# A hybrid decoder block in single precision: the second half of the tokens begins with the values of two heads, and three smaller edits

## The chip, the cores and the metric

The kernel runs on one core of one Trainium2 chip. A core has four engines that compute: TensorE (PE: matrix products and transposes into the accumulator memory PSUM), VectorE (DVE), ScalarE (ACT) and GpSimd (POOL). Transfers between the on-chip memory and DRAM are issued from the instruction queue of an engine; SyncE (SP) does nothing else. The metric is device time in microseconds (us), the median of several runs.

## The reference

One layer works on x of 1024 tokens x 2048 columns in float32:

```python
h = rmsnorm(x, ln_g)
proj = h @ w_in                    # columns for three groups and their gates
# group A: gMLP spatial gating in chunks of 128 tokens, 4 groups of 128
# group B: gated DeltaNet, 8 heads of 128: causal conv + SiLU on q, k, v;
#          per chunk T = (I + A)^-1, then a scan over the chunks carries a state
# group C: cross-attention into 256 memory tokens, 4 heads of 128
mixed = concat([out_a, out_b, out_c]) * SiLU(gates)
y = rmsnorm(x + mixed @ w_out, final_g)
```

The change lies in group B. For a head, `q`, `k` and `v` are each a projection of 128 columns, followed by a causal convolution of four taps. Inside a chunk the delta rule needs the inverse of a unit triangular matrix. The scan `S_t` runs over the tokens in order, so the second half of the tokens needs the state of the first.

## The kernel before, in words

**Precision.** Every product of the projections is done as three products (`triple`, line 445): an operand is split into a high part (`hi`, a rounded copy, made by ACT) and a low part (`lo`, the rest, made by DVE), and hi x hi, hi x lo and lo x hi are added in PSUM.

**Order of the work.** The program is first written down as a list of operations with their dependencies. `Plan.price` (line 182) gives each a cost and a latency, and `Plan.issue` (line 222) replays the list: each engine takes, of the operations that its prices call ready, the one of lowest rank (`with rank(n)`; matmuls of the projections have 9, the rest 5 unless said otherwise), and at equal rank the earlier in the program. The order found so is fixed, and every engine works through its own list in that order, waiting where a result isn't there yet. All instructions are issued from one line, so the profile shows line 277 (L277) for nearly everything; groups are told apart by tile names.

**Two halves of the tokens, heads 0 to 3.** The first 512 tokens of h lie split in `ahi` and `alo` (16 pieces of 128 rows each). In the first half heads 0 and 1 are projected (`front(0, 0)`, line 1138), then heads 2 and 3 (`front(1, 0)`), then the values of all four (`values`, line 1181). Each column of 128 is `project` (line 849): 16 pieces x 3 matmuls of 128 x 512 into one of two PSUM banks (`main_bank`), with weights loaded into the `wraw` ring of four and split into `whi` and `wlo` of five each (`w_parts`, line 830). `conv` (line 888) copies the bank into one of three `xr` buffers, so that the bank is free, and convolves from there: q into one of four `qT` slots, k into one of four `kT` slots, one for each head, values into one of four `tn` buffers.

**The chain of a pair of heads.** `qk` (line 924) makes the decays and the products k k and k q; it uses both `inv` buffers. `blocks_out` (line 967) writes 32 x 32 blocks to DRAM (`gdr`), `inverse` (line 980) loads them into an `inv` buffer, inverts 32 blocks at once with 31 steps of two DVE operations each (`y<-inv,inv` and `inv<-inv,y`), and writes the results to DRAM (`tdr`, `udr`). `levels` (line 1008) puts them together, and `scan_step` (line 1079) runs the four chunks. `back` (line 1191) is levels, the scan and `heads_out`. A pair's `qT` and `kT` slots are free for the other half when its scan is over. The inverse has rank 3, below the splits of operands, which have rank 2.

**The step to the second half** (lines 1216 to 1239). `refill` loads one piece of the second half's h from DRAM and splits it into `ahi` and `alo` as soon as the last column of the first half has used that piece. The first two columns of the second half are q and k of head 0, projected together, and each piece's refill and two matmuls of the decays stand ahead of their products (`before`, line 1225). Then follow `decays(1, a)`, the rest of `front(0, 1)` (q and k of head 1), the inverse "10", `back` of heads 2 and 3 of the first half, the values of heads 0 and 1, and heads 2 and 3 of the second half. Between columns `next_job` puts in one of the jobs of `todo`; here these are `left_sums`, which load, add and store pieces for a later stage.

**Low parts.** A column of weights is used in both halves. In `w_parts` the low part of a column of heads 2 and 3, and of the values of all heads, is stored in DRAM in the first half and loaded in the second; q and k of heads 0 and 1 are split anew.

**Later stages**, which the change touches only by the order and by the inverse's transfers: heads 4 to 7 and the other groups are projected in blocks with a scheme of seven products in place of eight (`seven`), the late inverse works on four pairs at once, and the output projection and the norm end the kernel.

Of the kernel before, what the change touches and what calls it, by code (L numbers as in the profile page):

```python
# [17 lines left out]
P = 128  # L18
# [44 lines left out]
class Plan:  # L63
# [117 lines left out]
    def price(self, o, name, outs, ins):  # L181

        out = outs[0]
        n = math.prod(out.shape[1:])
        both = [*outs, *ins]
        psum = any(i.space == PSUM for i in both)
        pointer = any(i.shape[-1] == 1 and math.prod(i.shape[1:]) == 1 for i in ins[1:])
        o.nbytes = o.lock = 0
        o.lat = 0.0
        if name == "dma_start":  # L190
            o.cost = {"sp": 380.0, "act": 100.0, "pool": 800.0}[o.eng]
            rows = math.prod(out.shape[:-1])
            o.nbytes = max(4 * math.prod(out.shape), 512 * rows)
            src = ins[0]
            pieces = src.shape[-1] < 128 or out.shape[-1] < 128
            if out.space == DRAM:
                o.lat = 3000.0
            elif pieces or out.shape[0] < 32:
                o.lat = 2400.0
            elif list(src.ap)[0][0] == 0:  # L200
                o.lat = 4000.0
        elif o.eng == "pe":
            passes = 1 if ins[0].dtype == F32R else 2 if name == "transpose" else 4
            o.cost = max(13.3 + n / 2.4 * passes, 110.0) if out.shape[0] == P else 30.0
            o.lat = 175.0
        elif o.eng == "act":
            o.cost = (165.0 if psum else 200.0) + 0.82 * n + (105.0 if pointer else 0.0)
            o.cost += 190.0 if "accum_out" in o.kw else 0.0
        elif o.eng == "dve":
            n = max([n] + [math.prod(i.shape[1:]) for i in ins])  # L210
            o.cost = (n + 151) / 0.96 + (60.0 if pointer and name == "scalar_tensor_tensor" else 0.0)
            o.lock = not psum and (name.startswith("tensor_") or name == "scalar_tensor_tensor")
            o.lock = o.lock and name != "tensor_reduce"
        else:
            o.lock = 1
            if name in ("memset", "affine_select"):
                o.cost = 100.0 + 0.83 * n * (1 if name == "memset" else 1.4)
                o.lat = 800.0 if name == "affine_select" else 0.0
            else:
                o.cost = 750.0 + 150.0 * (n - 1) if n < 8 else 200.0 + 2.1 * n  # L220

    def issue(self):
        free = dict.fromkeys(self.SEEN, 0.0)
        soon = {e: [] for e in free}
        now = {e: [] for e in free}
        held = {"dve": 0.0, "pool": 0.0}
        dma = 0.0
        for o in self.ops:
            if o.n == 0 and o.lead is o:
                heapq.heappush(soon[o.eng], (0.0, o.idx))  # L230
        left = len(self.ops)
        while left:
            best = None
            for e in free:
                if now[e]:
                    t = free[e]
                elif soon[e]:
                    t = max(free[e], soon[e][0][0])
                else:
                    continue  # L240
                if best is None or t < best[0]:
                    best = (t, e)
            t, e = best
            while soon[e] and soon[e][0][0] <= t:
                i = heapq.heappop(soon[e])[1]
                heapq.heappush(now[e], (self.ops[i].cls, i))
            head = self.ops[heapq.heappop(now[e])[1]]
            for o in (head, *head.tail):
                t = max(t, free[e])
                o.at = t  # L250
                left -= 1
                if o.lock:
                    t = max(t, held["pool" if e == "dve" else "dve"])
                end = t + o.cost
                if o.lock:
                    held[e] = end
                free[e] = end - min(self.OVERLAP[e], 0.5 * o.cost)
                done = end + o.lat
                if o.nbytes:
                    dma = max(dma, end) + o.nbytes / self.DMA_RATE  # L260
                    done = dma + self.DMA_FIXED + o.lat
                for s in o.succ:
                    if s.eng != e or o.nbytes:
                        when = done + self.SEEN[s.eng] + (self.SLACK if s.eng == "pe" else 0.0)
                    elif e == "pe":
                        when = free[e]
                    else:
                        when = end + 34.0
                    s.ready = max(s.ready, when)
                    s.n -= 1  # L270
                    if s.n == 0:
                        heapq.heappush(soon[s.eng], (s.ready, s.idx))
            if len(head.tail) > 7:
                free[e] += self.SWITCH
        self.ops.sort(key=lambda o: (o.at, o.idx))
        for o in self.ops:
            o.fn(*o.args, **o.kw)  # L277
# [3 lines left out]
def kernel(  # L281
# [543 lines left out]
            Q.dma_start(gcs[hf].rearrange("t h p -> (t h) p"), gr)  # L825


    low_d, todo = {}, []

    def w_parts(c0, kp):  # L830

        src = w_in[kp * KP * P : (kp + 1) * KP * P, c0 : c0 + P].rearrange("(k p) c -> p k c", p=P)
        raw = raw_piece(src)
        if (c0, kp) in low_d:
            hi, lo = whi(), wlo()
            with rank(2):
                S.copy(hi, raw)
            with rank(4):
                Q.dma_start(lo.bitcast(F32), low_d[c0, kp])
        else:  # L840
            hi, lo = split_piece(raw)
            if (c0 - C_Q) % DW < 2 * P and c0 < C_DV:
                return [tok(hi), tok(lo)]
            low_d[c0, kp] = DT([P, HT], f"low{c0}_{kp}")
            with rank(6):
                Q.dma_start(low_d[c0, kp], lo.bitcast(F32))
        return [tok(hi), tok(lo)]
# [40 lines left out]
    def conv(which, h, hf, o, a=None):  # L888
        ct = which * NH + h
        xr = ring["xr"]()  # L890
        w = [cw[:, k * 24 + ct : k * 24 + ct + 1] for k in range(4)]
        if h < NJ:
            if a is None:
                last = (which, h, hf) == (2, NJ - 1, 1)
                a = project([column(which, h)], order=(1, 0, 2, 3) if last else range(KT // KP))[0]
            next_job()
            with rank(1):
                S.copy(xr[:, 0:3], halo[:, ct])
                S.copy(xr[:, 3:], a)
# [12 lines left out]
        t = ring["tn"]()  # L912
        S.activation(t, o, AF.Tanh)
        V.scalar_tensor_tensor(o, t, 1.0, o, op0=ALU.add, op1=ALU.mult)
# [52 lines left out]
    def blocks_out(gt, n):  # L967
# [3 lines left out]
        for b in range(4):  # L971
            sl = slice(b * 32, (b + 1) * 32)
            with rank(1):
                Q.dma_start(gdr[b].rearrange("c j i -> j c i"), gv[sl, :, sl])
        return gdr

    def flat(start, *aps):
# [2 lines left out]
    def inverse(gdrs, n, cls):  # L980
# [3 lines left out]
        for i, gdr in enumerate(gdrs):  # L984
            for b in range(4):
                with rank(1):
                    flat(Q.dma_start, gd[i * 32 + b * 8 : i * 32 + (b + 1) * 8], gdr[b])
        ti = ring["inv"]()[0:nr].rearrange("p (a b) -> p a b", b=32)
        tmp = (y1 if nr == 32 else y2)[0:nr].rearrange("p c m -> p (c m)")
        with rank(4):  # L990
# [10 lines left out]
        tdr, udr = ([DT([32, 32, 32], f"{t}{n}_{i}") for i in range(len(gdrs))] for t in ("tdr", "udr"))  # L1001
        for i in range(len(gdrs)):
            with rank(1):
                flat(Q.dma_start, tdr[i], ti[i * 32 : (i + 1) * 32])
                flat(Q.dma_start, udr[i], gd[i * 32 : (i + 1) * 32])
        return list(zip(tdr, udr))

    def levels(gt, tdr, udr):
# [177 lines left out]
            by_token(rest[i][2], to_tokens((v, bank))[0], hss[i][:, 4])  # L1186

    def inverted(n, *states):
        return [(*s[:-1], i) for s, i in zip(states, inverse([s[-1] for s in states], n, 3))]

    def back(hf, hp, gt, qs, ks, hss, rest, inv, ut=None):
        ut = ut or levels(gt, *inv)
# [34 lines left out]
        decay_mm(a, k)  # L1227

    todo += [lambda j=j: left_sums(j) for j in range(NJ, NH)]
    first = project([column(0, 0), column(1, 0)], before)  # L1230
    decays(1, a)
    (state,) = inverted("10", front(0, 1, first))
    back(*ahead)
    ut = levels(state[2], *state[-1])
    values(*state)
# [545 lines left out]
```

## Time and profile before

| | us |
|---|---|
| three runs | 1644.93, 1648.33, 1648.26 (median 1648.26) |
| the profiled execution | 1647.33 |
| its span, from the first to the last instruction | 1645.6 |
| mean granted TensorE clock | 0.997 |

A row of busy time says how long an engine worked and the share of the span. Matmuls are pipelined: a product of 512 columns is shown with 0.39 us, and the next starts 0.23 us after it. A wait row has the engine that waited, what it waited for, the sum, the number of times and the longest. A window row has, for a stretch of the span, the busy time of PE, PEld (weight loads of TensorE), DVE, ACT and POOL, each with its number of instructions, then the granted clock, the DMA engines' share and GB/s. "SPq" and "ACTq" are the instruction queues of SyncE and ScalarE.

### The profile page before, as it was taken

To read this page: it belongs to the slowest core of one execution; us is meant where nothing else is said; L and a number is where in the kernel's file an instruction comes from. 1 tells how busy PE (TensorE), PEld (TensorE's weight loads), DVE (VectorE), ACT (ScalarE), POOL (GpSimd) and SP (SyncE) were. 2 spreads that over 40 slices of the span, in tenths; PEclk is the share of its full clock that TensorE was granted. 3 is DMA by queue.
4 is the path that set the end of the run, shared out by engine and by line. 5 is a ranking of instruction groups with operands and counts; after the bars stand their busy time and mean duration, and the time that the engine had idled before them with its cause. 6 is when DMAs were issued, how large, how long until landed. Compare 5 with 4: busy or idle time off the path is not lost.

```text
span 1645.6 us, 26195 instructions
## 1 busy us (share of the span) xinstructions
PE 1615.4 (98%) x8570; PEld 1354.1 (82%) x8570; DVE 1323.4 (80%) x2288; ACT 1025.8 (62%) x2235; POOL 117.1 (7%) x139
## 2 busy tenths in 40 slices
PE   8999999899999999999999999999999999999997
PEld 6888887788888888888888787888888888888886
DVE  4866796767879869899999898879678898688875
ACT  6957764576846446877686546766657774344445
POOL 0001110210200000100101101000000000000001
PEclk9999999999999999999999999999999999999999
DMA  8989888586887877579877887889778789678646
GB/s 265 257 233 278 261 275 258 178 247 200 265 287 238 265 236 231 183 266 331 303 229 243 293 277 208 276 281 303 249 240 279 258 281 352 200 269 300 220 143 241
DMA packets 316659, 419.51 MB, mean 255 GB/s; under 512 B 57773, under 2 KB 138342, under 8 KB 316522
## 3 DMA queue, kind: packets, MB, share of 16 engines
q1 hardware_dynamic: 314818, 414.67, 77.7%
q0 software_dynamic: 1088, 2.10, 0.5%
q8 instruction: 67, 1.10, 0.3%
q10 hardware_dynamic: 616, 1.07, 0.2%
q14 instruction: 70, 0.57, 0.1%
HBM read 334.33 MB, written 82.87 MB: 254 GB/s over the span
## 4 chain that ended last, share of the span: by engine, by line
PE 88%; DVE 4%; DMA 4%; issue 1%; ACT 1%; POOL 1%; SPq 0%; POOLq 0%; DVEq 0%; ACTq 0%
PE acc L277 67%; PE dn L277 21%; DMA wraw<-in_w_in_dram 1%; DVE alo L277 1%; DVE wlo L277 1%; DVE y L277 1%; DMA wraw<-hTd 1%; POOL hs L277 1%; DMA E<-gcd 0%; DMA sd<-zg 0%; ACT whi L277 0%; DVE kT L277 0%; DMA y<-in_w_in_dram 0%; SPq L277 0%; DMA el<-vd 0%
## 5 line engine op out<-in xcount | busy, mean ns | idle before, releaser
L277 PE MATMUL acc<-ahi,whi 128*128 128x512 f32 (+1 forms) x1152 | 453.0, 394 | 7.3 <-ACT xr L277 4.5
L277 PE MATMUL acc<-ahi,wlo 128*128 128x512 f32 (+1 forms) x1152 | 451.1, 392 | 0.4 <-DVE small L277 0.4
L277 PE MATMUL acc<-alo,whi 128*128 128x512 f32 (+1 forms) x1152 | 450.6, 391 | 0.0
L277 PEld LDWEIGHTS acc<-ahi,whi 128*128 128x128 f32 x1152 | 217.3, 189 | 49.7 <-ACT xr L277 5.2
L277 PEld LDWEIGHTS acc<-ahi,wlo 128*128 128x128 f32 x1152 | 217.3, 189 | 41.7 <-DVE small L277 0.6
L277 PEld LDWEIGHTS acc<-alo,whi 128*128 128x128 f32 x1152 | 217.4, 189 | 40.7
L277 PE MATMUL acc<-ahi,zh 128*128 128x512 f32 x736 | 234.6, 395 | 0.9 <-DVE gt L277 0.9
L277 ACT CAST whi<-wraw 128x512 fp32r<-128x512 f32 (+1 forms) x170 | 137.1, 808 | 105.6 <-PE acc L277 67.1
L277 DVE TENSOR_TENSOR alo<-raws,ahi 128x1024 fp32r<-128x1024 f32 x131 | 159.9, 1221 | 38.6 <-ACT ahi L277 37.3
L277 ACT CAST ahi<-raws 128x1024 fp32r<-128x1024 f32 x131 | 137.4, 1049 | 69.1 <-PE dn L277 28.2
L277 DVE TENSOR_TENSOR wlo<-wraw,whi 128x1024 fp32r<-128x1024 f32 (+1 forms) x138 | 134.4, 975 | 49.1 <-ACT whi L277 43.1
L277 PEld LDWEIGHTS acc<-ahi,zh 128*128 128x128 f32 x736 | 137.2, 188 | 27.9 <-DVE gt L277 1.1
L277 PE MATMUL acc<-ahi,zl 128*128 128x512 f32 x368 | 145.1, 394 | 0.0
L277 DVE TENSOR_TENSOR ahi<-y,ahi 128x1024 fp32r<-128x1024 f32 x65 | 79.3, 1220 | 20.5 <-ACT ahi L277 20.2
L277 ACT CAST ahi<-y 128x1024 fp32r<-128x1024 f32 x65 | 68.2, 1049 | 39.4 <-PE acc L277 21.8
L277 PEld LDWEIGHTS acc<-ahi,zl 128*128 128x128 f32 x368 | 69.3, 188 | 13.1
L277 POOL TENSOR_TENSOR hs<-hs,mhalf 128x4 f32<-128x4 f32 x32 | 54.7, 1711 | 229.8 <-DVE hs L277 223.3
L277 ACT CAST zh<-wraw 128x1024 fp32r<-128x1024 f32 x36 | 37.8, 1051 | 44.4 <-PE acc L277 27.6
L277 POOL TENSOR_TENSOR small<-small,mhalf 128x1 f32<-128x1 f32 x26 | 19.6, 757 | 577.1 <-DVE small L277 577.1
L277 PE MATMUL dn<-whi,alo 128*128 128x512 f32 x152 | 59.1, 390 | 0.0
L277 PE MATMUL dn<-wlo,ahi 128*128 128x512 f32 x152 | 59.0, 389 | 0.0
L277 PE MATMUL dn<-whi,ahi 128*128 128x512 f32 x152 | 58.9, 390 | 0.0
(397 smaller groups left out, 3201.5 us busy)
## 6 DMA issues: line engine op xcount, KB each, us to landing
wraw<-in_w_in_dram SPq DMA_DIRECT2D x268, 256.0 KB
raws<-sd SPq DMA_DIRECT2D x148, 256.0 KB
y<-in_w_in_dram SPq DMA_DIRECT2D x92, 256.0 KB
y<-sd SPq DMA_DIRECT2D x77, 256.0 KB
wraw<-in_w_out_dram SPq DMA_DIRECT2D x64, 256.0 KB
raws<-h0d SPq DMA_DIRECT2D x54, 256.0 KB
y<-in_w_out_dram SPq DMA_DIRECT2D x33, 256.0 KB
low<-wlo SPq DMA_DIRECT2D x32, 256.0 KB
```

The costliest lines, as they stand in the source:

```text
L277: o.fn(*o.args, **o.kw)
```

## The change

There are five edits.

1. The second half begins with the values of heads 0 and 1, projected together with the refill. Each bank is copied into a `tn` buffer and written to DRAM (`spilled`). Where `conv` is to make these values later, it loads them from DRAM into `xr` and projects nothing. All four columns of q and k of heads 0 and 1 are then projected one by one.
2. The rule for stored low parts: for the values of heads 0 and 1 they are no longer stored either; they are split anew in the second half, like q and k of these heads.
3. The transfers of `blocks_out` and `inverse` (`gdr`, the load into `inv`, `tdr`, `udr`) are issued from ACT's queue in place of SP's.
4. The first inverse ("00") has rank 1.9 in place of 3.
5. In the planner's prices, a full-precision matmul with 128 output rows costs at least 222 ns in place of 110, and transfers issued by ACT have an account of their own, at half the rate, beside that of the others.

```diff
-            o.cost = max(13.3 + n / 2.4 * passes, 110.0) if out.shape[0] == P else 30.0
+            o.cost = max(13.3 + n / 2.4 * passes, 222.0 if passes == 4 else 110.0) if out.shape[0] == P else 30.0
...
-                if o.nbytes:
+                if o.nbytes and e == "act":
+                    beside = max(beside, end) + 2 * o.nbytes / self.DMA_RATE
+                    done = beside + self.DMA_FIXED + o.lat
+                elif o.nbytes:
                     dma = max(dma, end) + o.nbytes / self.DMA_RATE
                     done = dma + self.DMA_FIXED + o.lat
...
-            if (c0 - C_Q) % DW < 2 * P and c0 < C_DV:
+            if (c0 - C_Q) % DW < 2 * P:
                 return [tok(hi), tok(lo)]
...
-        if h < NJ:
+        if h < NJ and (which, h, hf) in spilled:
+            S.copy(xr[:, 0:3], halo[:, ct])
+            Q.dma_start(xr[:, 3:], spilled[which, h, hf])
+            S.activation(o, xr[:, 3:], AF.Copy, scale=w[3])
+        elif h < NJ:
...
-                Q.dma_start(gdr[b].rearrange("c j i -> j c i"), gv[sl, :, sl])
+                S.dma_start(gdr[b].rearrange("c j i -> j c i"), gv[sl, :, sl])
...
-                    flat(Q.dma_start, gd[i * 32 + b * 8 : i * 32 + (b + 1) * 8], gdr[b])
+                    flat(S.dma_start, gd[i * 32 + b * 8 : i * 32 + (b + 1) * 8], gdr[b])
...
-                flat(Q.dma_start, tdr[i], ti[i * 32 : (i + 1) * 32])
-                flat(Q.dma_start, udr[i], gd[i * 32 : (i + 1) * 32])
+                flat(S.dma_start, tdr[i], ti[i * 32 : (i + 1) * 32])
+                flat(S.dma_start, udr[i], gd[i * 32 : (i + 1) * 32])
...
-        return [(*s[:-1], i) for s, i in zip(states, inverse([s[-1] for s in states], n, 3))]
+        return [(*s[:-1], i) for s, i in zip(states, inverse([s[-1] for s in states], n, 1.9 if n == "00" else 3))]
...
-    first = project([column(0, 0), column(1, 0)], before)
+
+    for h, bank in enumerate(project([column(2, 0), column(2, 1)], before)):
+        spilled[2, h, 1] = DT([P, HT], f"spill{h}")
+        t = ring["tn"]()
+        with rank(1):
+            S.copy(t, bank)
+        Q.dma_start(spilled[2, h, 1], t)
+        next_job()
     decays(1, a)
-    (state,) = inverted("10", front(0, 1, first))
+    (state,) = inverted("10", front(0, 1))
```

More of the change, by code (lines that the diff above doesn't have):

```diff
@@ L226, in issue @@
         held = {"dve": 0.0, "pool": 0.0}
-        dma = 0.0
+        dma = beside = 0.0
         for o in self.ops:
@@ L825, in decays @@
             Q.dma_start(gcs[hf].rearrange("t h p -> (t h) p"), gr)
-    low_d, todo = {}, []
+    low_d, todo, spilled = {}, [], {}
     def w_parts(c0, kp):
```

## The prediction

> **What bounds the kernel now.** I read the page's head first, then the chain that ended last, then what TensorE (PE) waited for in the stretch that the change rewrites (228 to 420 us), and last that stretch cut into windows.
>
> ```profile
> span 1645.6 us, 26195 instructions
> PE 1615.4 (98%) x8570; PEld 1354.1 (82%) x8570; DVE 1323.4 (80%) x2288; ACT 1025.8 (62%) x2235; POOL 117.1 (7%) x139
> ...
> PE 88%; DVE 4%; DMA 4%; issue 1%; ACT 1%; POOL 1%; SPq 0%; POOLq 0%; DVEq 0%; ACTq 0%
> ```
>
> PE is busy 98% of the span and carries 88% of the closing chain. The change alters no product of the projections, so it can win only what PE stands idle, 1645.6 - 1615.4 = 30.2 us, or runs at a lower clock. Two tables say how much of that lies where the change acts.
>
> ```profile
> PE acc L277 <- ACT xr L277: 4.5, 2, 2.8
> PE dn L277 <- ACT vs L277: 2.5, 2, 1.6
> PE acc L277 <- ACT whi L277: 0.9, 1, 0.9
> PE acc L277 <- DVE tn L277: 0.3, 1, 0.3
> PE dn L277 <- ACT steps L277: 0.2, 1, 0.2
> ```
>
> ```profile
> core 0: us, PE busy (x) PEld busy (x) DVE busy (x) ACT busy (x) POOL busy (x), PEclk, DMA share, GB/s
> 309.00:316.00 7.00, 4.18 (x17) 3.35 (x16) 6.44 (x16) 5.02 (x18) 1.42 (x1) 0.76 0.67 199
> 228.00:253.00 25.00, 23.31 (x106) 18.70 (x104) 23.27 (x48) 14.17 (x27) 0.00 (x0) 1.00 0.81 252
> 253.00:289.00 36.00, 35.67 (x250) 29.85 (x250) 20.93 (x47) 15.40 (x37) 2.77 (x4) 1.00 0.80 242
> 289.00:313.00 24.00, 20.98 (x130) 18.30 (x129) 21.07 (x78) 11.47 (x42) 0.20 (x1) 0.99 0.79 240
> ```
>
> The waits of 228 to 420 us add to 4.5 + 2.5 + 0.9 + 0.3 + 0.2 = 8.4 us. The longest, 2.8 us, has a second price: in 309 to 316 us the granted clock is 0.76, so 7 x 0.24 = 1.7 us more of PE's time are gone. Both belong to one event, which the timeline shows.
>
> ```profile
> 309.51 0.39 PE L277 MATMUL dn<-steps,ai 128*128 128x128 f32 x2
> 312.72 0.80 PE L277 MATMUL acc<-ahi,whi 128*128 128x512 f32 x1 [2.81 <-ACT xr L277]
> ```
>
> ```profile
> 252.70 1.06 ACT L277 COPY xr<-acc 128x512 f32<-128x512 f32 x2
> ...
> 264.89 0.58 ACT L277 COPY xr<-acc 128x512 f32<-128x512 f32 x1
> ...
> 306.76 0.73 ACT L277 ACTIVATE kT<-xr,cw 128x512 f32<-128x512 f32 x1 [1.44 <-PE dn L277]
> ...
> 312.08 0.58 ACT L277 COPY xr<-acc 128x512 f32<-128x512 f32 x1
> ```
>
> Projections fill two PSUM banks in turn, and a full bank is emptied into one of three xr buffers. The second half's q0, k0 and q1 are emptied at 252.70 (two) and 264.89 and hold all three. Their convolutions need the qT and kT slots of heads 0 and 1, which the first half's scan holds until its last step (matmuls up to 309.51). So k1 and v0 stay in the two banks, and PE stops until k1's bank is emptied at 312.08. **PE can go five columns past the half's start before the scan of heads 0 and 1 must be over**, and that was 3 us too few.
>
> **The change part by part.** *Values first.* The first two columns of the second half become v0 and v1. They go to two tn buffers and by DMA to DRAM, and need neither xr nor a slot. After them come q0, k0, q1 (xr), k1 and q2 (banks): seven columns instead of five. A column is 48 matmuls, with 0.23 us between starts:
>
> ```profile
> 401.15 0.39 PE L277 MATMUL acc<-alo,whi 128*128 128x512 f32 x1
> 401.38 0.39 PE L277 MATMUL acc<-ahi,wlo 128*128 128x512 f32 x1
> ```
>
> So two columns are 2 x 48 x 0.227 = 22 us of cover against a lack of 2.8: the stop goes, and its clock dip. Term: **-2.8 - 1.7 = -4.5 us**. The two copies (0.58 us each, as xr's) replace the xr copies of v0 and v1; reading the spills adds two loads, hidden by 100 us of distance. The wait of 1.7 us at 251 (4.5 - 2.8) stays, as two banks again fill in the same matmul: term 0, bounds -1.7 and +1.7.
>
> What is late next is the last column, v3, which needs the bank of k3. That was emptied at 399.39, and v3 began at 401.38, with 401.38 - 399.39 - 0.58 = 1.4 us to spare:
>
> ```profile
> 399.39 0.58 ACT L277 COPY xr<-acc 128x512 f32<-128x512 f32 x1
> ```
>
> If PE comes 4.5 us earlier and the scan of heads 2 and 3 doesn't, 4.5 - 1.4 = 3.1 us are given back there. That scan hangs on the first two inverses, the next part.
>
> *First inverse ahead of splits* (rank 1.9 for 3, splits have 2).
>
> ```profile
> L277 DVE TENSOR_TENSOR y<-inv,inv x31: 172/349/405, 203.1 to 262.2; 32x31 f32<-32x31 f32 x2, 32x60 f32<-32x60 f32 x2, 32x87 f32<-32x87 f32 x2, 32x112 f32<-32x112 f32 x2
> L277 DVE TENSOR_TENSOR inv<-inv,y x31: 179/346/407, 203.3 to 262.4; 32x31 f32<-32x31 f32 x2, 32x60 f32<-32x60 f32 x2, 32x87 f32<-32x87 f32 x2, 32x112 f32<-32x112 f32 x2
> ...
> L277 DVE TENSOR_TENSOR wlo<-wraw,whi 128x512 fp32r<-128x512 f32 x7 | 4.8, 679 | 0.9 <-ACT whi L277 0.9
> L277 DVE TENSOR_TENSOR zg<-zg,zg 128x512 f32<-128x512 f32 x3 | 2.0, 673 | 0.0
> ```
>
> Its 62 dependent operations of about 0.35 us take 59 us (203.1 to 262.4). They still cannot run back to back: when one ends its successor isn't ready, and one waiting operation of 0.67 us gets in. In the worst stretch that is about 1.0 us a step. I estimate an end 8 us earlier, from 0.35 + 0.67 against the 59 / 62 and more that the later steps take. It brings the next inverse forward as much, since front(1, 0) waits for its inv buffers. That is set against the added splits: v0 and v1 no longer have kept low parts, so 8 splits of 0.68 us = 5.4 us come in where VectorE (DVE) has 36 - 20.93 = 15 us free (253 to 289). Even if all 5.4 came off, 8 - 5.4 = 2.6 us stays, against 3.1 wanted. I take **0** for the give-back, bounds 0 and +3.1. The price of the early inverse is in 228 to 253, when PE eats the refilled tokens as they come and DVE has 25 - 23.27 = 1.7 us free. Left sums (zg, rank 6, 2.0 us there) and convolutions (rank 5) yield first, so a refill split waits at most one operation of 0.35. Term **0**, bounds -0.3 (the tn wait above) and +7.2, worked out as a rival.
>
> *Kept low parts.* Heads 0 and 1 of the values leave 8 stores and 8 loads out:
>
> ```profile
> L277 SPq DMA_DIRECT2D low<-wlo x32: 336/531/1371, 120.2 to 215.4; - x32
> L277 SPq DMA_DIRECT2D wlo<-low x32: 319/358/490, 265.2 to 399.1; - x32
> ```
>
> That is 8 x (0.53 + 0.36) = 7 us of SyncE's queue (SP) and 16 x 256 KB of transfers; 4 x 256 KB of spill come back. DMA is at 0.80 in those windows and no wait above names it: term 0, bounds -0.9 (the whi wait) and 0.
>
> *Inverse transfers on ScalarE's queue (ACT).*
>
> ```profile
> L277 SPq DMA_DIRECT2D gdr<-gt x32: 303/448/2274, 187.1 to 907.0; - x32
> L277 SPq DMA_DIRECT2D inv<-gdr x32: 263/293/588, 195.2 to 913.1; - x32
> ...
> L277 ACTq DMA_DIRECT2D zg<-in_ln_g_dram x4: 229/256/523, 1.3 to 4.1; - x4
> ```
>
> Eighty issues move: 32 + 32 of these and 16 of tdr and udr. ACT already issues at 0.26 (zg row); with SP's times one early inverse costs ACT 4 x 0.45 + 4 x 0.29 + 2 x 0.43 = 3.8 us, where the planner counts 1.0. Behind a waiting issue stand casts of weights, the copies that empty banks, and the scan's copies. The whi ring holds five pieces of 12 matmuls, 5 x 12 x 0.227 = 13.6 us of PE work, and covers the casts. The scan's copies have the 0.6 us slack of the plan. I take 2.8 us late, shared over four inverses mostly beside cover, as **+0.5 us** in all, nearest to the 0.2 us that PE waits for steps now; bounds 0 and 4 x (2.8 - 0.6) = +8.8.
>
> *Price list.* The 222 ns for small matmuls and the separate account of ACT's transfers run nowhere on the chip: they reorder instructions. Term 0, bounds by the shortest and longest PE waits above, -2.8 and +2.8.
>
> The 1.64 us that PE waits for vs near 324 us is a POOL operation:
>
> ```profile
> 314.58 1.72 POOL L277 TENSOR_TENSOR hs<-hs,mhalf 128x4 f32<-128x4 f32 x1 [12.08 <-DVE hs L277]
> 317.04 6.62 POOL L277 TENSOR_TENSOR hs<-hs,mhalf 128x4 f32<-128x4 f32 x1 [0.75 <-DVE hs L277]
> ```
>
> The same operation takes 1.72 or 6.62 us. The long one runs while DVE works off the convolutions that the scan's end sets free, and that burst stays: term 0, bounds -1.6 and 0. The Trainium skill, "GPSIMD Engine Reference", section "1. Specifications", says that GpSimd shares its SBUF interfaces with VectorE and contends with VectorE instructions of two SBUF inputs. By that rule the burst makes this wait again and the sum keeps it, which agrees with these two rows; were the long run an accident, the sum would be 1.6 us lower.
>
> **Sum.** -4.5 + 0.5 = -4.0 us. The profiled execution took 1647.33 us (span 1645.6 and 1.7 around it), inside the three runs' 1644.93 to 1648.33 and 0.9 under their median of 1648.26. Forecast **1643.3 us**.
>
> **The rivals.** *More goes than one wait*: the whole 8.4 us and the 1.7 of clock, because everything behind the first inverse comes earlier: 1647.3 - 10.1 = 1637.2. For it: four of the five waits hang on that chain or on SP. Against: the POOL rows.
>
> *Given back at v3*: the scan of heads 2 and 3 isn't earlier, and 3.1 us return: 1643.3 + 3.1 = 1646.4. For it: 1.4 us to spare and more splits; against: DVE's 15 us free.
>
> *Refill starved* (slower): at 228 to 253 the early inverse displaces not left sums but token splits. From 249 us on 23 of its 62 operations were still to run:
>
> ```profile
> L277 DVE TENSOR_TENSOR inv<-inv,y x12: 179/316/387, 248.8 to 262.4; 32x240 f32<-32x240 f32 x1, 32x231 f32<-32x231 f32 x1, 32x220 f32<-32x220 f32 x1, 32x207 f32<-32x207 f32 x1
> L277 DVE TENSOR_TENSOR y<-inv,inv x11: 173/307/381, 250.2 to 262.2; 32x231 f32<-32x231 f32 x1, 32x220 f32<-32x220 f32 x1, 32x207 f32<-32x207 f32 x1, 32x192 f32<-32x192 f32 x1
> ```
>
> Pulled ahead of the refill they are 12 x 0.316 + 11 x 0.307 = 7.2 us of PE idle, with 1.7 of clock: 1643.3 + 7.2 + 1.7 = 1652.2. It decides once the inverse work drawn into that window exceeds the 1.7 us free plus what left sums and convolutions can yield. For it: 23.27 of 25 us; against: the plan lets one split through after each step.
>
> *ACT blocked* (slower): its issues wait for DVE's inverse or for landings and hold up the scan's copies, +8.8 for +0.5: 1651.6. Against: ACT is busy 62%, and the plan asks for data late.
>
> **How the numbers follow.** About 0.2%, 3.3 us, is what a measurement of this kernel can tell from no change. Forecast 0.42 (with the reordering's 2.8 either way, 0.30 of it faster by over 3.3 and 0.12 within), more goes 0.15 (faster), given back 0.19 (0.17 within, 0.02 slower), refill starved 0.14 and ACT blocked 0.10 (slower). Faster 0.45, same 0.29, slower 0.26. The range goes from the best case, 1637, to the starved refill, 1652; the forecast's own case is 1640.5 to 1646.1.
>
> **What would show it.** Right: no wait of PE for xr of 2 us or more between 289 and 330 us, and a clock of 1.00 there; first inverse over by about 254 us; PE waits for ACT of at most 0.6 us beside the scans; 24 stores and 24 loads of low. Wrong: a PE gap on refilled tokens at 228 to 255, or ahead of v3 near 395, or a clock dip in a new place.

## The result, and the profile after

The changed kernel took **1672.57 us** (median of five runs, 1671.36 to 1677.68) against 1648.33 for the kernel before (five runs): ratio **1.0145**, interval 1.0119 to 1.0172. Forecast were 1643.3 us and a range of 1637 to 1652. The change made the kernel slower by 24 us, and the prediction was wrong in sign. Of the five edits, the third decides: the transfers of the inverse issued by ACT.

The head of the page of the changed kernel and the shares of the chain that ended last:

```profile
span 1669.6 us, 26192 instructions
PE 1626.0 (97%) x8570; PEld 1358.5 (81%) x8570; DVE 1322.1 (79%) x2296; ACT 1023.9 (61%) x2235; POOL 102.6 (6%) x139
...
PE 76%; DMA 9%; DVE 7%; issue 3%; ACT 2%; SPq 1%; ACTq 0%; POOL 0%; POOLq 0%; DVEq 0%
```

PE does the same 8570 products. Its idle time rose from 30.2 to 1669.6 - 1626.0 = 43.6 us, and it was busy 10.6 us longer for the same work, which is mostly a matter of the clock (below). 13.4 + 10.6 are the 24.0 us of the span. ACT is as busy as it was (61% for 62%), so a glance at shares shows no culprit; only the chain tells that PE's part fell from 88 to 76% and DMA's rose from 4 to 9%.

What PE waited for between 228 and 420 us, the stretch that the prediction worked on:

```profile
PE dn L280 <- ACT steps L280: 4.1, 1, 4.1
PE dn L280 <- issue: 1.2, 2, 0.8
PE acc L280 <- ACT whi L280: 0.9, 1, 0.9
PE acc L280 <- ACT tn L280: 0.6, 1, 0.6
PE acc L280 <- ACT xr L280: 0.4, 1, 0.4
```

The two waits for xr, 4.5 us before, are down to one of 0.4: the stop that the change aims at is gone. A new wait of 4.1 us for ACT stands in its place, and over the whole span there are more like it (rows of the same view; the row of `in_mem_dram` is as before):

```profile
PE dn L280 <- ACT gt L280: 7.3, 2, 5.2
PE dn L280 <- ACT vs L280: 5.4, 1, 5.4
PE dn L280 <- DMA kT<-in_mem_dram: 4.8, 1, 4.8
...
PE dn L280 <- ACT inv L280: 2.3, 1, 2.3
```

Five stops, 7.3 (two) + 5.4 + 4.1 + 2.3 = 19.1 us, all for a result of ACT. Windows around them, then one of a smaller stop at 1012 us, and last the window of the old stop; first after, then the same stretches before:

```profile
core 0: us, PE busy (x) PEld busy (x) DVE busy (x) ACT busy (x) POOL busy (x), PEclk, DMA share, GB/s
366.00:376.00 10.00, 5.87 (x26) 4.86 (x25) 1.92 (x5) 2.64 (x9) 0.00 (x0) 0.83 0.99 330
489.00:502.00 13.00, 7.61 (x32) 5.88 (x31) 7.49 (x16) 6.66 (x15) 0.00 (x0) 0.74 0.83 285
688.00:697.00 9.00, 6.66 (x29) 5.40 (x29) 5.40 (x9) 5.60 (x15) 0.00 (x0) 0.81 0.74 230
891.00:908.00 17.00, 9.66 (x29) 6.88 (x28) 9.73 (x16) 8.63 (x12) 0.00 (x0) 0.70 0.84 275
1009.00:1018.00 9.00, 7.44 (x33) 5.82 (x32) 5.54 (x11) 6.65 (x13) 1.62 (x2) 0.81 0.85 279
309.00:316.00 7.00, 7.00 (x33) 5.78 (x32) 6.04 (x15) 5.80 (x22) 4.34 (x2) 1.00 0.69 216
```

```profile
366.00:376.00 10.00, 10.00 (x58) 8.66 (x58) 1.12 (x4) 5.09 (x14) 0.00 (x0) 1.00 0.66 197
489.00:502.00 13.00, 13.00 (x64) 10.86 (x63) 10.26 (x19) 10.62 (x26) 2.41 (x2) 1.00 0.96 322
688.00:697.00 9.00, 9.00 (x42) 7.45 (x41) 8.81 (x15) 6.49 (x14) 1.98 (x2) 1.00 0.68 209
891.00:908.00 17.00, 14.70 (x67) 11.75 (x65) 15.28 (x26) 8.25 (x12) 4.49 (x4) 1.00 0.70 216
1009.00:1018.00 9.00, 9.00 (x90) 7.39 (x89) 7.18 (x11) 6.96 (x14) 0.88 (x1) 1.00 0.43 98
```

In the first four windows PE is idle 4.13 + 5.39 + 2.34 + 7.34 = 19.2 us after, and 2.3 before. By the clock records of the trace the granted clock, 1.00 before, is at one half there for 3.4, 6.8, 3.4 and 10.2 us; PE worked during 19.0 of these 23.9 us, and at half the clock that costs it 9.5 us more. Net that is 16.9 + 9.5 = 26.4 us lost. The stop at 1012 us adds 1.6 and 1.7 of clock; it stands behind a load of SP that ACT needs, and it is also there with the transfers on POOL (2.7 us in g2_plan_pool below), so it isn't part of this. The window of 309 us gives the forecast 4.5 us back (PE 7.00 of 7.00 at 1.00). 26.4 + 3.3 - 4.5 = 25.2 against the 24.0 us of the span: **the loss lies in these four places**, and what came and went elsewhere nearly cancels. The runs g1 and g2 test this at one and the same order.

What ACT did there is in its timeline (a row with ACTq is the issue of a transfer, with its start and length; in brackets the idle time of ACT ahead of its next result):

```profile
370.47 0.27 ACTq L280 DMA_DIRECT2D inv<-gdr  x1
370.78 0.37 ACT L280 COPY ut<-dn 64x256 f32<-64x256 f32 x1 [5.54 <-DMA sd<-zg]
...
490.27 2.45 ACTq L280 DMA_DIRECT2D inv<-gdr  x2
492.81 0.62 ACT L280 CAST whi<-kT 128x512 fp32r<-128x512 f32 x1 [6.41 <-DMA inv<-gdr]
...
687.57 3.04 ACTq L280 DMA_DIRECT2D gdr<-gt  x4
690.66 0.40 ACT L280 ACTIVATE E<-E,sc 128x128 f32<-128x128 f32 x1 [3.21 <-issue]
...
888.49 3.56 ACTq L280 DMA_DIRECT2D gdr<-gt  x4
892.09 1.05 ACT L280 CAST whi<-wraw 128x1024 fp32r<-128x1024 f32 x1 [5.56 <-issue]
...
901.16 0.27 ACTq L280 DMA_DIRECT2D inv<-gdr  x1
901.47 0.59 ACT L280 COPY gt<-acc 128x512 f32<-128x512 f32 x1 [3.31 <-DMA raws<-sd]
```

Each of the five stops stands behind a transfer of the inverse on ACT. ACT computes nothing for 3 to 6 us, then works off what stands behind the transfer, and with it the result that PE wants. Two things are to be seen. Four issues in a row take 3.0 and 3.6 us, though the median of all 32 is 0.46 (shortest, median and longest in ns):

```profile
L280 ACTq DMA_DIRECT2D gdr<-gt x32: 309/462/1672, 190.3 to 891.0; - x32
L280 ACTq DMA_DIRECT2D inv<-gdr x32: 269/282/588, 197.7 to 901.2; - x32
```

And the load at 370.47 was held up by `sd<-zg`, the one at 901.16 by `raws<-sd`: transfers of SP that share no tile with the inverse. The semaphore numbers in the trace say why. SP and ACT mark the end of their transfers on the same eight semaphores in turn (100 to 107; in the kernel before SP has 218 to 220 transfers on each). The load at 370.47 has number 103; the one before it on 103 was SP's `sd<-zg` of 363.75. It is issued 0.02 us after the last update of that semaphore, at 370.45. The load at 901.16 has number 106, and so has the one at 490.27, whose row names only its own kind: there too the older transfer is a `raws<-sd` of SP (issued at 483.52, last update 490.25). In all three the newer transfer is not issued before the older one on its semaphore has landed. In g2_plan_pool, where the record of three of the eight semaphores is complete, the same holds for all 621 pairs of transfers that follow each other on one of them.

### The profile page after: what moved, and what is told of

It reads as the page before. It is cut to its first block, busy times and chain, and to the rows that moved or that the text cites. A ratio compares the mean times of both kernels' runs of the same rounds, so it can differ in the third digit from the quotient of the medians.

```text
span 1669.6 us, 26192 instructions
## 1 busy us (share of the span) xinstructions
PE 1626.0 (97%) x8570; PEld 1358.5 (81%) x8570; DVE 1322.1 (79%) x2296; ACT 1023.9 (61%) x2235; POOL 102.6 (6%) x139
## 4 chain that ended last, share of the span: by engine, by line
PE 76%; DMA 9%; DVE 7%; issue 3%; ACT 2%; SPq 1%; ACTq 0%; POOL 0%; POOLq 0%; DVEq 0%
PE acc L280 56%; PE dn L280 20%; DMA wraw<-in_w_in_dram 1%; DVE wlo L280 1%; DVE y L280 1%; DVE alo L280 1%; DMA gdr<-gt 1%; SPq L280 1%; DMA zg<-hTd 1%; DMA raws<-sd 1%; ACT whi L280 1%; DVE wraw L280 1%; DMA wraw<-hTd 1%; DVE inv L280 1%; DVE ai L280 0%
## 5 line engine op out<-in xcount | busy, mean ns | idle before, releaser
L280 DVE TENSOR_TENSOR wlo<-wraw,whi 128x1024 fp32r<-128x1024 f32 (+1 forms) x146 | 140.4, 962 | 62.8 <-ACT whi L280 53.4
L280 ACT CAST whi<-y 128x1024 fp32r<-128x1024 f32 x34 | 35.7, 1050 | 39.9 <-issue 20.4
L280 DVE TENSOR_TENSOR wlo<-y,whi 128x1024 fp32r<-128x1024 f32 x34 | 41.5, 1220 | 22.4 <-ACT whi L280 22.2
```

## The experiments

Theory: ACT works its list in order, so a transfer that must wait holds up the copies behind it; that is the loss. Rivals: the values at the front (edits 1 and 2), the early inverse, and the new order itself.

Any edit lets the planner find another order, which is a change by itself. In the kernels whose name has "plan", and in g3 and h1, the order is held (in their traces DVE and ACT work through the same instructions one by one as the kernel that they start from, but for g7's added copies): the transfers stay planned for the engine they had and only their issue is sent elsewhere, by

```
Z = Engine(R, "act", nc.gpsimd)   # planned as ACT's, issued by POOL
...
Z.dma_start(gdr[b]...)            # in the four places of edit 3
```

All ratios are to the kernel before, with 95% interval.

**e1_sp**, the changed kernel without edit 3:

```
-  S.dma_start(gdr[b]...)   # and the loads into inv, tdr, udr
+  Q.dma_start(gdr[b]...)
```

> The changed kernel with one edit undone: the 80 transfers of the inverses are issued by SP again (values first, low parts, rank 1.9 and the prices stay). My theory: the 24 us are ScalarE standing in order behind its own transfers, each of which first waits for the completion semaphore of an earlier transfer (eight semaphores are shared by SP and ScalarE in turn); then this kernel loses nearly all 24 us and comes to 1640 to 1650 us, and PE's waits for ScalarE of over 2 us at 367, 490, 689, 893 and 1010 us are gone. Rival, the new order: values first, the early inverse or the prices make the loss; then it stays at 1665 us or more.

Measured: 1.0085 (1.006 to 1.0111). Taking the transfers off ACT gets back four tenths of the loss. The planner's order is another here, with a stop of its own (PE waits 8.8 us for ACT's `zh`, up to 433.5 us, early in the stage of blocks), so the rest could be the values or the order. By its time (1666.18 us) it lies where the rival put it; the order is untangled from the queue by g1 and g2.

**e2_act**, the kernel before with edit 3 alone (the same lines, `Q` to `S`):

> The kernel before with that one edit alone: the 80 transfers are issued by ScalarE, everything else as before, prices too. My theory: slower by 15 to 25 us, 1663 to 1673 us, with waits of ScalarE of 2 to 6 us right ahead of its transfers. Rival, the new order: 1648 us, no change. Rival, only together: slower by under 8 us.

Measured: 1.0127 (1.0098 to 1.0155). Edit 3 alone, with the order that the planner then finds, makes nearly the whole loss; g3 repeats it at the order of the kernel before.

**e3_tiny**, e1_sp and 80 stores of 512 bytes from ACT:

```
+  with behind(op):
+      S.dma_start(scrap[i : i + 1], ident[0:1])
```

> As e1_sp (inverse transfers on SP), with 80 stores of 512 bytes added to ScalarE's queue at the same places, from a constant to a scratch area that nobody reads, so that they wait for no data. It tells why a transfer on ScalarE's queue costs time. My theory, the shared semaphores: ScalarE still waits 1 to 5 us ahead of some of them, and the kernel is slower than e1_sp by 6 to 20 us. Rival, the wait for data (the load into inv waits until the blocks have landed): under 2 us slower than e1_sp. Rival, the issue itself (80 x 0.3 = 24 us of ScalarE): ScalarE has no wait over 1 us ahead of these stores, and the loss is some 2 to 8 us in small pieces.

Measured: 1.0131 (1.0103 to 1.0158), 7.4 us over e1_sp, in the range of the theory and of the rival of the issue time alike. Only one of the stores stood over 1 us on ACT (1.46 us), which spoke for the issue time and against the shared semaphores. But the planner had put everything in a new order; g4 and g7 make the trial again at one order and turn this reading round.

**e4_pool** and **e4_again**, the changed kernel with `G.dma_start` (POOL) for `S.dma_start` in edit 3, planned as POOL's:

> The changed kernel with the 80 transfers issued by GpSimd (POOL) in place of ScalarE. POOL is busy 6% and little stands behind its transfers. My theory: in-order blocking of ScalarE is the cost, so this kernel is fast too, 1640 to 1655 us, with waits on POOL's queue that PE doesn't feel. Rival, a second queue beside SP's makes the small transfers themselves slow (blocks land 5 us after issue in place of 1 to 2): then the chain of the inverse is late here too and it stays over 1662 us.

> The changed kernel with the inverse's 80 transfers issued from POOL and planned there, a second time and with more rounds. If its gain stands: 0.995 to 0.999 of before; if it was chance, the interval holds 1.

Measured: 0.9975 (0.9958 to 0.9991) and 0.9979 (0.9964 to 0.9993), median 1647.3 and 1648.64 us: **faster than both kernels**, by a quarter of a per cent against the kernel before. PE's longest waits in 250 to 420 us:

```profile
PE acc L280 <- ACT xr L280: 4.1, 1, 4.1
PE acc L280 <- ACT whi L280: 0.9, 1, 0.9
```

The stop at 310 us is gone, and 4.1 us come back at 392.2 us, where v3 wants the bank of k3: the rival "given back at v3". The rival of the slow small transfers had its condition right: by the trace of g2_plan_pool a block stored by POOL lands 5.6 us after its issue (median of 32), where one of SP's lands 2.7 us after it in the kernel before (by the last update of its semaphore). Its price didn't come.

**f1_values**, the kernel before with edits 1 and 2 alone (values first, transfers on SP):

```
-    first = project([column(0, 0), column(1, 0)], before)
+    for h, bank in enumerate(project([column(2, 0), column(2, 1)], before)):
+        spilled[2, h, 1] = DT([P, HT], f"spill{h}")
...
```

> The kernel before with the first two edits alone: the second half begins with the values of heads 0 and 1, and their low parts aren't stored. My prediction's step: the stop of 2.8 us at 310 us and its half clock go, 4.5 us faster, 1643 to 1646 us. Rival, given back at the last column before the block stage, a wait of 3 us or more for xr at 390 to 402 us: 1646 to 1650 us. Rival, the new order opens a gap where the block stage begins (419 to 435 us in e1_sp, 13 us and 13.7 us of half clock): 1660 us or more.

Measured: 1.0064 (1.0046 to 1.0082). PE's waits in 250 to 420 us:

```profile
PE dn L277 <- DVE states L277: 5.7, 1, 5.7
PE acc L277 <- ACT xr L277: 4.3, 1, 4.3
PE acc L277 <- ACT tn L277: 2.4, 1, 2.4
```

The old stop is gone and is paid back twice: at 403.7 us for k3's bank (4.3), and at 374.5 us inside the scan of heads 2 and 3 (5.7). At 1664.01 us it lies in the range of the third rival, but the gap at 419 to 435 us that this rival names isn't there. The aim of the change by itself wins nothing here; how much of the 0.64% is the order isn't shown (f2 to j1 say how much an order can be worth).

**g1_plan_sp, g2_plan_pool**: the changed kernel's order on every engine, its transfers issued by SP (`nc.sync` in the line above) or by POOL:

> The changed kernel with the order of every engine's instructions held as it is: the 80 transfers are planned as ScalarE's, priced as such, but stand on SP's queue at the same point of the plan. Only the queue differs, not the order, which differed in e1_sp too. If ScalarE's standing behind its transfers is the loss: back to 1640 to 1652 us, and PE's waits of over 2 us at 367, 490, 689 and 893 us are gone. If the order is the loss: 1665 us or more, with PE's waits at the same places for something else.

> As g1_plan_sp, but on POOL's queue. If ScalarE's standing is the loss: 1640 to 1655 us. If a second queue beside SP's makes the small transfers slow and the chain late: over 1660 us, with ScalarE out of it.

Measured: SP 1.0053 (1.0035 to 1.007), POOL **1.0002** (0.9985 to 1.002). With nothing else changed, 1.4% goes when the transfers leave ACT for POOL, and the changed kernel is then as fast as the kernel before. SP, at 1661.86 us, lies between the two ranges expected: 0.9% goes, and 0.5% against POOL stays, with PE's longest new waits for DVE's `steps` (4.4 us) and `ai` (3.6) and for loads of the inverse's results (2.8 and 2.3). Why SP is late with them in this order isn't shown. The four windows, with POOL:

```profile
366.00:376.00 10.00, 7.64 (x44) 6.33 (x43) 2.78 (x10) 3.36 (x11) 1.20 (x3) 1.00 0.97 325
489.00:502.00 13.00, 13.00 (x66) 10.91 (x65) 9.87 (x26) 9.63 (x20) 0.00 (x0) 1.00 0.98 345
688.00:697.00 9.00, 8.11 (x39) 6.53 (x38) 6.74 (x11) 9.00 (x26) 1.61 (x2) 1.00 0.80 279
891.00:908.00 17.00, 17.00 (x79) 14.05 (x78) 17.00 (x31) 7.19 (x8) 0.00 (x0) 1.00 0.56 170
```

PE is idle 2.36 + 0.89 = 3.3 us in them for 19.2, at a clock of 1.00. As this kernel gets ahead, the later windows hold later work. A fairer comparison takes the matmuls one by one, since their order is the same in both: the changed kernel is 1.3 us ahead of g2 at 366 us of its own time and 4.7 behind at 376, 1.8 and 9.9 behind at 489 and 502, 10.5 and 13.9 at 688 and 697, 14.4 and 25.3 at 891 and 908. It loses 6.0 + 8.1 + 3.4 + 10.9 = 28.4 us in the four windows, and is 24.5 us behind at 1600: they hold the whole loss. POOL itself stands for the inverse's results, up to 62.5 us, and PE has no wait for POOL (us in all, times, longest):

```profile
POOL tdr L280 <- DVE inv L280: 112.8, 4, 62.5
```

**g3_before_act, h1_before_pool**: the other way round, the order of the kernel before, its transfers issued by ACT or by POOL:

```
+    Z = Engine(R, "sp", nc.scalar)    # h1: nc.gpsimd
```

> The kernel before with the order of every engine held as it is, and the 80 transfers on ScalarE's queue at the same point of the plan (planned and priced as SP's). If ScalarE's standing is the loss: slower by 12 to 25 us. If the loss of e2_act came from the plan that the other price makes: within 5 us of before.

> The order of the kernel before on every engine, without the change; only the 80 transfers go from POOL's queue in place of SP's. Theory (the queue matters where its engine has other work behind the transfer, and POOL has next to none): 0.997 to 1.002 of before, while the same order with them on ACT took 1.0114. Rival (SP's queue was itself late with the big loads behind these transfers): faster, 0.990 to 0.996, and the fast version of the changed kernel with POOL's queue then owes its gain to the queue alone.

Measured: ACT 1.0114 (1.0081 to 1.0147), POOL 0.9994 (0.9976 to 1.0012). ACT's price stands in both orders, and POOL's queue by itself gains nothing over SP's in this order.

**g5_plan_loads, g6_plan_stores**: g2, with the 32 loads on ACT alone, or the 48 stores:

```
-  flat(Z.dma_start, gd[i * 32 + b * 8 : ...], gdr[b])
+  flat(S.dma_start, gd[i * 32 + b * 8 : ...], gdr[b])   # g5; g6: the other three
```

> The changed kernel's order on every engine; only the 32 loads of the blocks (inv<-gdr) stay on ACT, the 48 stores (gdr, tdr, udr) go from POOL's queue. Theory 'waits for a landing' : the loads wait for the store of the blocks to land, so they carry most of the loss, 1.008 to 1.014 of before. Rival 'waits for a result or mere number': loads are 32 of 80, 40% of the 1.4 per cent, 1.004 to 1.007.

> The changed kernel's order on every engine; only the 48 stores (gdr, tdr, udr) stay on ACT, the 32 loads go from POOL's queue. Theory 'waits for a landing': little, 1.000 to 1.005 of before. Rival 'waits for a result or mere number': 60% of the loss, 1.007 to 1.010.

Measured: loads 1.0079 (1.0058 to 1.0099), stores 1.0057 (1.0039 to 1.0075). Neither expectation holds alone: both kinds cost, over g2 0.77 and 0.55%, together 1.32 of 1.43. By these figures a load costs about twice as much as a store (0.024 and 0.011% each); the intervals of the two runs overlap, so the factor is rough.

**g4_plan_tiny, g7_plan_copy**: g2, and at each of the 80 places ACT issues a tiny store, or makes a small copy:

```
 class Both:
     def dma_start(self, dst, src):
         nc.gpsimd.dma_start(dst, src)
+        nc.scalar.dma_start(self.scrap[self.n : self.n + 1], ident[0:1])   # g4
...
+        nc.scalar.copy(jk[:, 0:96], ident[:, 0:96])                        # g7
```

> The order of every engine is that of the changed kernel; the 80 real transfers go from POOL's queue, and beside each of them ACT issues, at the same place of its order, a store of 512 bytes of a constant to a scratch row in DRAM, which waits for no result (what is computed is unchanged). Theory 'waits' (ACT stands behind transfers whose data or landing isn't there yet): only the issue time remains, 80 x 0.26 = 21 us of ACT, mostly beside cover, so the time is near that of the same order with the transfers on POOL, 1.000 to 1.005 of before. Rival 'issue' (80 more instructions of ACT in its order cost it, whatever they wait for): near the changed kernel, 1.010 to 1.015.

> The changed kernel's order with the 80 transfers on POOL, and at each of their places ACT makes a copy of 128 x 96 elements to a scratch tile: about as long as issuing a transfer (0.2 to 0.3 us each, 80 of them 16 to 24 us of ACT) and waiting for nothing (what is computed is unchanged). With a tiny store in the copy's place it was 1.0053 of before, without either 1.0002. Theory 'completions': the tiny stores cost what they do because a store waits until an older transfer of SP with the same completion semaphore has landed; the copy doesn't, so 0.999 to 1.003. Rival 'time of ACT': 1.004 to 1.007.

Measured: stores **1.0053** (1.0034 to 1.0073), copies **0.9991** (0.9976 to 1.0005). 80 more pieces of work are free to ACT (its busy time rose by 1041.2 - 1024.3 = 16.9 us from g2 to g7); 80 stores that need no result are not. The group of these stores, and the one that stood longest:

```profile
L322 ACTq DMA_DIRECT2D scrap<-ident x80: 221/222/1502, 187.5 to 970.6; - x80
```

```profile
491.87 0.22 ACTq L322 DMA_DIRECT2D scrap<-ident  x1
492.19 0.62 ACT L280 CAST whi<-kT 128x512 fp32r<-128x512 f32 x1 [2.97 <-DMA E<-gcd]
```

A constant went to a scratch row, and still ACT stood idle 2.97 us, 2.6 of them until `E<-gcd` had landed, a load that SP had issued at 484.03 on the same semaphore (105). Eight of the 80 stores stood over 1 us, 12.6 us in all, and each of the eight was issued within 0.03 us of the last update that an older transfer of SP made on its semaphore. That the price isn't ACT's time is what g7 shows; that it is these waits is read from the trace, and no run takes the shared semaphores away by themselves.

**f2_rank, f3_price, j1_nudge**: the kernel before with edit 4 alone, with the matmul price of edit 5 alone, and with a price that means nothing:

```
-  inverse([s[-1] for s in states], n, 3)
+  inverse([s[-1] for s in states], n, 1.9 if n == "00" else 3)   # f2
-  max(13.3 + n / 2.4 * passes, 110.0)
+  max(13.3 + n / 2.4 * passes, 222.0 if passes == 4 else 110.0)  # f3
-  o.cost = {"sp": 380.0, ...
+  o.cost = {"sp": 385.0, ...                                     # j1
```

> The kernel before with the fourth edit alone (rank 1.9 of the first inverse). Theory 'order': some of the cost that the changed kernel has even without its transfers on ACT comes from here, PE waiting on refilled tokens at 228 to 255: 1.003 to 1.006 of before. Rival: the early inverse is free or brings the scans forward: 0.997 to 1.001.

> The kernel before with the fifth edit alone (222 ns as the price of the small matmuls in the planner; nothing on the chip runs otherwise, only the order changes). Theory 'order': another order alone moves the time by more than the 2.8 us that were allowed: below 0.998 or above 1.002 of before. Rival: within 1 +- 0.0015.

> The kernel before, unchanged but for the planner's price of a transfer issued by SP, 385 ns in place of 380, which means nothing for the chip and only shifts the order. Theory 'picked order' (the order of before is the best of many, and any other order costs some tenths of a per cent): 1.002 to 1.006 of before, like the early inverse alone (1.0046) and the price of small matmuls alone (1.0043). Rival (these two edits cost what they do by what they mean): 0.998 to 1.0015.

Measured: f2 1.0046 (1.0031 to 1.0062), f3 1.0043 (1.0026 to 1.0059), j1 **0.9976** (0.9961 to 0.999). "Picked order" falls: a price of 5 ns more, without meaning, made the kernel faster, as much as e4_pool, with the stop at 310 us still in it. Another order is worth anything from -4.0 us (j1, 0.0024 x 1648) to +7.6 (f2). f2 came out as its theory said, but PE waits only 1.1 us at 228 to 255 us, where the theory put the cost. Its longest wait, below, comes 170 us after the early inverse; that of f3 (second) is in a matmul whose price the edit raises:

```profile
437.09 0.80 PE L277 MATMUL dn<-states,kT 128*128 128x128 f32 x2 [6.31 <-ACT jk L277]
```

```profile
379.47 1.30 PE L277 MATMUL dn<-states,kT 128*128 128x128 f32 x4 [4.15 <-ACT vs L277]
```

**e5_three**, e4_pool with a third column of values made ahead:

```
...
+    spill(2, project([column(2, 2)])[0])
```

> As the changed kernel with the transfers on POOL, but the values of head 2 are made ahead and kept in DRAM as well (a third spill, the column after the first two). Theory 'given back': the stop at 392 us (4.1 us for xr and a half-clock stretch of 3.4 us) comes because the last column needs the bank of the column before it; with one value column fewer at the end it finds a free bank, so 4.1 + 1.7 = 5.8 us go: about 0.994 of before and 0.0035 under the same kernel with two spills. Rival: the scan of heads 2 and 3 ends where it did and the stop only moves to the next stage: no difference to two spills.

Measured: 1.0035 (1.0019 to 1.0052). It takes the stop at 392 us away, and that doesn't pay: neither the theory nor the rival came true. Windows of e5, then of e4:

```profile
388.00:400.00 12.00, 12.00 (x65) 10.24 (x64) 10.53 (x28) 7.75 (x27) 2.79 (x2) 1.00 0.38 121
470.00:510.00 40.00, 30.81 (x222) 26.04 (x222) 19.57 (x45) 19.75 (x62) 8.42 (x14) 0.77 0.46 124
```

```profile
470.00:510.00 40.00, 39.72 (x212) 33.32 (x211) 30.10 (x57) 21.57 (x55) 8.10 (x12) 1.00 0.79 250
```

PE now works through 388 to 400 us, and stands 9.2 us in 470 to 510, at 0.77 of the clock (up to another 9.2): the second half's scan of heads 0 and 1 runs there. One order differs from the other in more than the column, so that the column is the reason for the second stop is argued, not shown.

## Why the prediction was wrong, point by point

- **Values first, -4.5: right in the stop, wrong as a gain.** No wait for xr over 0.4 us in the stretch, clock 1.00 in 309 to 316 us. But the whole change with its transfers on POOL, at the changed order, takes as long as the kernel before (1.0002), so the 4.5 us are lost again elsewhere.
- **Give-back at v3, taken as 0, bounds 0 and +3.1: too low where it came.** 4.1 (e4_pool) and 4.3 us (f1_values) come back there, with a dip of the clock behind them. In the changed kernel it doesn't show; PE has lost 4.1 us at 367 us, ahead of it. Nor does it in g2_plan_pool, where PE waits 2.4 us for `steps` at 375 us. The scan of heads 2 and 3 was over at 393.3 us before and at 394.2 after (last product `dn<-steps,ai`), with the stop of 367 us inside it; without that stop it was over at 392.4 (g2_plan_pool) and 391.0 us (e4_pool), and with the early inverse alone at 392.2 (f2_rank). In these orders the scan came 0.9 to 2.3 us earlier, less than the 3.1 that were wanted.
- **First inverse: the size a little off, the price right.** It ended at 256.5 us, 6 us earlier and not 8: its operations took 49 us for 59, but began 4 us later (207.2 for 203.3). The starved refill did not come (no stop over 1 us in 228 to 253 us).

```profile
L280 DVE TENSOR_TENSOR inv<-inv,y x31: 171/340/409, 207.2 to 256.5; 32x31 f32<-32x31 f32 x2, 32x60 f32<-32x60 f32 x2, 32x87 f32<-32x87 f32 x2, 32x112 f32<-32x112 f32 x2
```

- **Wait at 251 us, and the wait for POOL, both 0.** The first fell from 1.7 to 0.6 (the row of `tn`); the second went, and with it 1.6 us, the far end of its bounds: the two POOL operations together took 4.34 us where one alone had taken 6.62.
- **Low parts, 0:** 24 stores and 24 loads, and no wait between 228 and 420 us names them.
- **Inverse transfers on ACT, +0.5, bounds 0 and +8.8: this step failed.** It costs 1.0145 - 1.0002 = 1.43% or 23.6 us against POOL, 0.92% or 15.2 us against SP, and 1.14% or 18.8 us in the order of before: 15 to 24 us for 0.5. The rival "ACT blocked" named the right mechanism with a chance of 0.10 and a third to a half of its price. Three things were missed. The step counted issue times and granted only 2.8 us of lateness to an inverse, and not the time for which a transfer can stand: 3 to 6 us at each of five stops. It counted only the early four inverses, and two of the four windows (689 and 891 us) lie in the later ones, with 7.34 of the 19.2 us idle in the last. And it gave no price to the clock, which added 9.5 us to 19.2.
- **Order, 0, bounds -2.8 and +2.8: bounds too narrow.** The longest wait of one order says nothing of the waits of another. f3 gives +0.43% (7.1 us), j1 -4.0 us.

How much of ACT's price is what: copies 0; 80 stores that need no result, about 0.5 to 0.6% (g4 over g2 and g7), which fits their waits for older transfers by way of the shared semaphores; the remaining 0.8 to 0.9% comes with the real transfers. In the changed kernel's trace (stands of over 0.15 us) ACT stands ahead of its transfers for 26.5 us, in 20 places, until an older transfer of SP on the same semaphore has landed (16.2 us in 15 places with the tiny stores), and 8.8 us for other things, mostly the result to be stored. The coupling also runs the other way: SP stands 7.3 us, in five places, for transfers of ACT, and never with the tiny stores. Longer issues come on top. How the 0.8 to 0.9% divides between these the runs don't tell apart. Nor is it shown whether the gain of e4_pool has to do with its values or is a lucky order like j1's.

The Trainium skill, "DMA: Bandwidth & Descriptors", section "Issuing engines are not separate DMA queues", says that starting transfers from several engines saves only the time that a sequencer needs to start one. The runs agree that there was little to win: POOL in place of SP is worth nothing in the order of before (0.9994), and 0.5% in the changed one.

## What to carry to other kernels

Before a transfer is moved to the queue of an engine that computes, list what stands behind each one in that engine's order, and price the longest time that it can stand there (its data, the landing of older transfers with the same semaphore, a row of issues), at all places in the kernel, with the clock that PE loses after a stop; an engine with nothing urgent behind it can wait for free. When an edit lets a planner choose again, compare at a held order first, and try a price without meaning too, since that alone moved this kernel by -0.24%. Here a stop whose buffer hangs on a scan was moved by more cover and not removed (e4_pool, f1_values): look where the next buffer of the kind is wanted.

## What was not expected of the hardware

- SP's and ACT's transfers use the same eight completion semaphores in this program, so a 512-byte store from ACT stood 2.6 us for a load of SP. POOL's use eight others (111 to 118): a transfer there doesn't stand behind SP's.
- POOL was the best place to issue from, though it takes longer to issue there (median 0.586 us for a block of `gdr`, against 0.46 on ACT) and the block lands later (5.6 us after its issue, against 2.7 on SP in the kernel before):

```profile
L280 POOL DMA_DIRECT2D gdr<-gt x32: 582/586/785, 190.3 to 871.7; - x32
```

The Trainium skill, "SBUF — State Buffer", section "🔬 SBUF: two separate sides", warns that transfers issued from POOL starve while DVE runs an operation that holds the port it shares with POOL, such as a float32 copy within SBUF. How much of DVE's work here is of that kind isn't shown; at 80% of DVE, POOL was 1.0002 against 1.0053 for SP and 1.0145 for ACT at one order, so whatever starving there was cost less here than the other two queues did.

- Short stops already cost clock: a stop of PE of 2.3 us up to 692 us was followed by 3.4 us at half clock (0.81 in 688 to 697 us), and one of 1.6 us up to 1012 us likewise (0.81 in 1009 to 1018). Not every one is: after 2.4 us at 1035 us in f1_values the clock stayed at 1.00.
